# A decoder layer on one core: the place of the cache multiplications, the order and key layout of the prompt scores, and the spacing of x in SBUF

## The chip, the cores and the metric

The kernel runs on one core of a Trainium2 chip. That core has five engines with queues of their own: TensorE (PE, with the weight loads PEld), VectorE (DVE), ScalarE (ACT), GpSimd (POOL) and SyncE (SP, which here only issues DMAs). The metric is the device time of one execution in microseconds (us); lower is better. The kernel before takes 1733.12 us, the median of three runs.

## The reference

One inference step of one decoder layer, for a prompt of 256 tokens and for 8 samples of 4 tokens each, 288 tokens in all, width 2048, all in fp32. The two groups share the weights. Cut to what matters:

```
z = x @ w_in                       # h, gate_b, gate_c, q, k, v, g_a, g_b from one projection
ya = gate_b * conv3(gate_c * h)    # mixer A
for g, (window, dilation) in enumerate(((128, 1), (512, 4), (2048, 16))):
    out[g], lse[g] = banded_attention(q[g], k[g], v[g], slopes[g], dilation)   # mixer B, 4 heads of 128
yb = sum(softmax(lse over g)[g] * out[g] for g in range(3))
x1 = layernorm(ALPHA*x + (sigmoid(g_a) * (ya @ w_branch_a) + sigmoid(g_b) * (yb @ w_branch_b)) @ w_out)
a, b = split(x1 @ w_up)
y = layernorm(ALPHA*x1 + (silu(conv3(a)) * b) @ w_down)
```

In the prompt, a query of dilation group g meets only keys whose distance is a multiple of the dilation. The samples attend to cached keys and values (2048 positions in the widest group, of which a token needs every 16th). Results are y, the new convolution states and the new caches.

## The kernel before, in words

All activations are kept with features on the partitions: x is a tile of 128 partitions by 16 k-tiles by 288 token columns. To keep fp32 precision, each operand is split in a high and a low part (`split`, L228: ACT copies the high part to fp32r, DVE subtracts it). A product of 128 output features (`product`, L204, `mms`, L217) is a sum over the k-tiles of three matmuls: high weights with high x (L223), high weights with low x (L224), low weights with high x (L225). 303 weight blocks pass through in this way, most of them with 16 k-tiles, 48 matmuls.

Weights flow like this: `prepare` (L179) issues the load of a 1 MB block to one of three `wst` buffers on SP's queue and splits it in two halves of 8 k-tiles (`half_block`, L153), each to one of four `whi` and one of four `wlo` buffers. `w_split` holds the two instructions of the last split made, `w_load[0]` the last load.

The order of the products is: queries, keys and values of the heads, the three parts of mixer A, the two gated branches, w_out, and the feed-forward in three thirds. Other work is slipped in between products:

- `sample_events` (L472) is a list of (product number, action). `cache_load` (L446) issues the load of one of 18 cache tiles of 1 MB each for keys (`ck`) and values (`cv`) on SP's queue, behind the last weight load, `LEAD` products ahead of its use, to one of three `cache` buffers. The tiles 2 to 17 of each are due `TILE_K` or `TILE_V` products apart, in two halves; `weighted` (L451) multiplies a half by queries or probabilities (four `activation`s on ACT at L460, one multiplication on DVE at L464) and reduces it (DVE, L466).
- `prompt_attention` (L353) is a generator; its first stage runs right after a head's last value product. POOL first sorts the values of the groups 1 and 2 by class, that is by position modulo 4 (`v_cls`, L359). PE then computes, for each of two query blocks, the scores of group 0 (L367: 128 or 256 columns) and those of groups 1 and 2 by class (L373: 32-column stationary parts, keys read from the key tile with a step of four elements, that is 16 bytes). Two products later the values and probabilities are transposed, and one product later multiplied.

A scheduler places the instructions on their engines: it sorts them by a simulated timeline, keeping dependences. `behind` (L141) adds an order between two instructions that carries no semaphore. So where the program names an action, and where it stands in an engine's queue, can differ. Every engine works its queue off in order: an instruction that waits holds all behind it.

x is held in `xh` and `xl` (L244): each k-tile has two halves of the columns, `HX` = 145 elements each, 144 of which are tokens, and matmuls take an element from each half in turn. The 145th column of the first third of the feed-forward carries the norm's gain and bias (`x_gb`, matmuls of 290 columns); there are 32 such products, and 169 products with 288 columns of x. `yah` and `yal`, the operands of most other products, hold 288 columns in one piece per k-tile.

The functions that the change touches, and what calls them:

Of the kernel before, what the change touches and what calls it, by code (L numbers as in the profile page):

```python
# [12 lines left out]
F32R = mybir.dt.float32r  # L13
AF = mybir.ActivationFunctionType
ALU = mybir.AluOpType
# [3 lines left out]
P = 128  # L19
D = 2048  # L20
KD = D // P
SEQ = 256
NB, NT = 8, 4
# [5 lines left out]
H = T // 2  # L29
HG = H + 1  # L30
HX = 145
FF = 5632
KF = FF // P
HK = KD // 2
THIRDS = (16, 16, 12)
NG, NH = 3, 4
# [10 lines left out]
NM = NG * P  # L47
NC = 4
# [29 lines left out]
SQ = 32  # L78
# [1 line left out]
TILE_K = 2.75  # L80
VALUES_AT = 64
TILE_V = 2.5
LEAD = 7

# [9 lines left out]
def layer_kernel(ctx: ExitStack, tc: tile.TileContext, ins, outs):  # L96
    nc = tc.nc
    pe, dve, act, pool, sp = nc.tensor, nc.vector, nc.scalar, nc.gpsimd, nc.sync

    big = ctx.enter_context(tc.tile_pool(name="big", bufs=1))  # L100
# [6 lines left out]
    def nm(s):  # L107
        uid[0] += 1
        return f"{s}_{uid[0]}"

    def sb(pl, shape, tag, dt=F32, bufs=None):
        return pl.tile(shape, dt, tag=tag, name=nm(tag), bufs=bufs)
# [4 lines left out]
    def h2(ap):  # L117
        return ap.rearrange("p (h a) -> p h a", h=2)

    def h3(ap):  # L120
        return ap.rearrange("p k (h a) -> p k h a", h=2)
# [5 lines left out]
    def att(cols=512):  # L127
        return sb(ps, [P, cols], "att", bufs=2)
# [12 lines left out]
    def behind(i, after):  # L141

        tc.add_manual_dep(i.ins, after.ins.name, no_sync, reason="pace")
# [7 lines left out]
    w_split = []  # L151
# [89 lines left out]
        pe.matmul(o, zero[:, :P], zero, start=True, stop=True)  # L241


    xh = sb(big, [P, KD, 2, HX], "xh", F32R)  # L244
    xl = sb(big, [P, KD, 2, HX], "xl", F32R)
    x_in = ins["x"].rearrange("p (k t) -> p k t", t=T)
    xs = sb(big, [P, KD, T], "yah")

# [8 lines left out]
    for k0, n, queue in FIRST:  # L257
        k = slice(k0, k0 + n)
# [4 lines left out]
    for k0, n, _ in FIRST:  # L263
        k = slice(k0, k0 + n)
        splits.append(split(xh[:, k, :, :H], xl[:, k, :, :H], xs[:, k].rearrange("p k (a h) -> p k h a", h=2)))
        h = slice(k0 % HK, k0 % HK + n)
# [34 lines left out]
    pa = sb(big, [P, KD * T], "yal")  # L301

    m_dist = [pa[:, :NM], pa[:, NM : 3 * NM]]
    v_cls = pa[:, 3 * NM : 3 * NM + 2 * 2 * P].rearrange("p (c k) -> p c k", c=NC)
    q_0 = pa[:, 3 * NM + 4 * P : 3 * NM + 6 * P].rearrange("p (b k) -> p b k", b=2)
    pa_at = [3 * NM + 6 * P]

    def pa_take(n):
        pa_at[0] += n
        return pa[:, pa_at[0] - n : pa_at[0]]  # L310

    v_two = [pa_take(2 * NG * P).rearrange("p (b d) -> p b d", d=P) for _ in range(2)]
    s_two = [pa_take((b + 2) * P) for b in range(2)]
    xs_flat = xs.rearrange("p k t -> p (k t)")
    q_all = xs_flat[:, : NH * NG * T].rearrange("p (j g t) -> p j g t", j=NH, g=NG)
# [32 lines left out]
    def in_a_row(row):  # L348

        for before, i in zip(row, row[1:]):  # L350
            behind(i, before)

    def prompt_attention(j, qT, kT, vT):  # L353


        q5 = h3(qT)[:, :, :, :P].rearrange("p g r (b u c) -> p g b r c u", b=2, c=2)
        k5 = kT[:, 1:, :SEQ].rearrange("p g (b u c r) -> p r c b g u", b=2, c=2, r=2)
        for g in range(1, NG):
            pool.tensor_copy(  # L359
                v_cls.rearrange("p c (b g u) -> p g c b u", b=2, g=2)[:, g - 1],  # L360
                vT[:, g, :SEQ].rearrange("p (b u c) -> p c b u", b=2, c=NC),
            )
        s3 = [att((b + 1) * P + (b + 1) * 2 * SQ) for b in range(2)]
        row = [last_mm[0]]
        for b in range(2):
            n = (b + 1) * P
            row.append(pe.matmul(s3[b][:, :n], q_0[:, b], kT[:, 0, :n], start=True, stop=True))  # L367
            by_class = s3[b][:, n:].rearrange("p (b g u) -> p g b u", g=2, u=SQ)
            for g in range(1, NG):
                for r in range(2):  # L370
                    for c in range(2):
                        at = slice(SQ * (2 * r + c), SQ * (2 * r + c + 1))
                        row.append(pe.matmul(  # L373
                            by_class[at, g - 1], q5[:, g, b, r, c], k5[:, r, c, : b + 1, g - 1], start=True, stop=True
                        ))
        in_a_row(row)
        s = [s_two[b][:, : (b + 1) * (P + 2 * SQ)] for b in range(2)]
        for b in range(2):
            n = (b + 1) * P
            dve.scalar_tensor_tensor(  # L380
                s[b][:, :n], m_dist[b][:, :n], -SLOPE[0][j] / SCALE, s3[b][:, :n], ALU.mult, ALU.add
            )
            dst, src = (t[:, n:].rearrange("p (b g u) -> p g b u", g=2, u=SQ) for t in (s[b], s3[b]))
            for g in range(1, NG):
                m = m_dist[b][:, g * n : (g + 1) * n].rearrange("p (b u c) -> p b u c", u=SQ, c=NC)[:, :, :, 0]
                dve.scalar_tensor_tensor(dst[:, g - 1], m, -SLOPE[g][j] / SCALE, src[:, g - 1], ALU.mult, ALU.add)
        for b in range(2):
            st = sb(wk, [P, 4], "st", bufs=4)
            dve.reduce_max(st[:, 0:1], s[b], AX.X)
            dve.tensor_scalar_mul(st[:, 1:2], st[:, 0:1], -SCALE)  # L390
            act.activation(s[b], s[b], AF.Exp, bias=st[:, 1:2], scale=SCALE, accum_out=st[:, 2:3])
            dve.reciprocal(st[:, 3:4], st[:, 2:3])
            dve.tensor_scalar_mul(s[b], s[b], st[:, 3:4])
        yield 2
        v = v_two[j % 2]
        pv = [att(NG * P) for _ in range(2)]
        row = [last_mm[0]]
        for n in range(2 * NG):
            out = pv[n // NG][:, n % NG * P : (n % NG + 1) * P]
            src = vT[:, 0, n * P : (n + 1) * P] if n < 2 else v_cls[:, n - 2]  # L400
            row.append(pe.transpose(out, src, ident))
        for n in range(2):
            act.copy(v[:, n * NG : (n + 1) * NG], pv[n].rearrange("p (b d) -> p b d", d=P))
        pt = [sb(ps, [P, (b + 2) * P], "acc") for b in range(2)]
        in_a_row(row + [
            pe.transpose(pt[b][:, c * P : (c + 1) * P], s_two[b][:, c * P : (c + 1) * P], ident)
            for b in range(2) for c in range(b + 2)
        ])
        for sT, t in zip(sT_two, pt):
            act.copy(sT, t)  # L410
        yield 1
        po = att(2 * P)
        row = [last_mm[0]]
        row.append(pe.matmul(h2(po), v[:, 0], sT_old, start=True, stop=False))
        row.append(pe.matmul(po[:, P:], v[:, 1], sT_two[1][:, P : 2 * P], start=False, stop=False))
        for c in range(NC):
            at = slice(c * SQ, (c + 1) * SQ)
            row.append(pe.matmul(
                h2(po)[:, :, at], v[:, 2 + 2 * (c % 2) + c // 2], sT_cls[:, :, at], start=False, stop=c == NC - 1
            ))  # L420
        in_a_row(row)
        o_b = oT.rearrange("p (r b u c) -> p b r c u", r=2, b=2, c=2)
        for b in range(2):
            act.copy(o_b[:, b], po[:, b * P : (b + 1) * P].rearrange("p (r c u) -> p r c u", r=2, c=2))
        split(h2(ybh[:, j])[:, :, :P], h2(ybl[:, j])[:, :, :P], oT.rearrange("p (h a) -> p h a", h=2))
# [25 lines left out]
    def weighted(which, n, half, w):  # L451

        c, (g, b) = cache_tiles[which, n], divmod(n - 2, NB)
        cols = NT * P
        for j in (2 * half, 2 * half + 1):
            e = c[:, j * cols : (j + 1) * cols]
            if j % 2 == 0:
                for t in range(NT):
                    e_t = e[:, t * P : (t + 1) * P]
                    act.activation(e_t, e_t, AF.Copy, scale=w[:, g + 1, j, b * NT + t : b * NT + t + 1])  # L460
            else:
                e3 = e.rearrange("p (t k) -> p t k", t=NT)
                w3 = w[:, g + 1, j, b * NT : (b + 1) * NT].unsqueeze(2).broadcast_to([P, NT, P])
                dve.tensor_tensor(e3, e3, w3, ALU.mult)  # L464
        j = slice(2 * half, 2 * half + 2)
        dve.tensor_reduce(  # L466
            parts[:, g, :, j, b * NT : (b + 1) * NT].rearrange("p k j t -> p j t k"),
            c[:, 2 * half * cols : (2 * half + 2) * cols].rearrange("p (j t k c) -> p j t k c", j=2, t=NT, c=SQ),
            AX.X, ALU.add, apply_transpose=True,
        )  # L470

    def sample_events():  # L472
# [98 lines left out]
        for which, w, first, apart in (("ck", q_s, SCORES_AT, TILE_K), ("cv", sT_w, VALUES_AT, TILE_V)):  # L571
            for n in range(N_CT):
                at = first + n if n < 2 else first + 2 + (n - 2) * apart
                yield at - LEAD, partial(cache_load, which, n)
                if n < 2:
# [32 lines left out]
    for j in range(NH):  # L608
        kT, vT = (kv[:, j % 2, c] for c in range(2))
# [58 lines left out]
    for i in range(KD):  # L668
        ph = product(x)
        h = sb(wk, [P, T], "h", bufs=2)  # L670
        act.copy(h2(h), ph)
        pc = product(x)
        u = sb(wk, [P, UW + 2], "u", bufs=2)
# [176 lines left out]
    for part, nf in enumerate(THIRDS):  # L850
        gh = sb(big, [P, KD, T], "yah", F32R)
        gl = sb(big, [P, KD, T], "yal", F32R)
        for k in range(nf):
            pa = product(x_gb if part == 0 else x)
            u = sb(wk, [P, UW + 2], "u", bufs=2)
            up, us = conv_in(u[:, :UW], R_SF + f * 2 * NB)
            if part == 0:
                pa, b1 = normed(pa)
# [227 lines left out]
```

## Time and profile before

| what | us |
|---|---|
| median of three runs (lowest, highest) | 1733.12 (1732.72, 1734.83) |
| the profiled execution | 1734.33 |
| its span, first to last instruction | 1732.5 |
| first matmul of the first three products after the span's start | 9.4 |
| first scores of the four heads, after the span's start | 116.0, 156.1, 196.1, 236.2 |

The profile is that of one execution. Its rows are read like this: a group row gives line, engine, operation, destination and sources by the program's names, shape, count, then busy us and mean ns of one, then idle time of the engine before them and what ended it. In the instructions in order of time the first two columns are start and duration, and brackets hold idle time before the row and its releaser; neighbours of one kind are merged (x8). A list of waits has who waited for what, the total us, how often, and the longest. A row of a stretch has its bounds and length and, for each engine, busy time and instruction count, then the granted clock, the share of the DMA engines and GB/s. A matmul's record covers its way through the array, so records overlap: the pace is read from start to next start, and the end is modelled. A matmul with both operands in plain fp32 has two records.

### The profile page before, as it was taken

How to read it: one execution, taken by the hardware profiler on the slowest of the kernel's cores; microseconds unless marked ns; L12 is line 12 of the kernel's file. 1: busy time of each engine (PE TensorE's matmuls, PEld its weight loads, DVE VectorE, ACT ScalarE, POOL GpSimd, SP SyncE). 2: the span in 40 equal slices, each digit the busy share in tenths (PEclk: the TensorE clock that was granted, in tenths of full speed). 3: DMA queues.
4: the chain of work that ended last, by engine and by line, in shares of the span. 5: the costliest groups of instructions: out<-in, count | busy, mean ns of one | idle time of the engine just before them, and what ended most of it. 6: DMA issues, size and time to landing. Idle time of an engine off the chain costs nothing.

```text
span 1732.5 us, 33671 instructions
## 1 busy us (share of the span) xinstructions
PE 1712.0 (99%) x14102; PEld 1703.6 (98%) x14102; DVE 1100.5 (64%) x1406; ACT 866.8 (50%) x1402; POOL 259.3 (15%) x420
## 2 busy tenths in 40 slices
PE   9999999999999999999999999999999999999996
PEld 9999999999999999999999999999999999999996
DVE  5485667658766654455688888765555554555554
ACT  5455555446555543344445655544454443344444
POOL 0001010000010000011364333300111100011165
PEclk9999999999999999999999999999999999999998
DMA  9676665565666766688766676666676666766652
GB/s 348 231 264 262 240 240 219 209 240 213 263 243 246 294 267 245 247 312 295 306 249 246 259 273 243 257 254 246 259 273 247 261 246 249 273 256 255 241 202 96
DMA packets 57656, 436.16 MB, mean 252 GB/s; under 512 B 7648, under 2 KB 9696, under 8 KB 17632
## 3 DMA queue, kind: packets, MB, share of 16 engines
q1 hardware_dynamic: 55776, 429.29, 65.2%
q10 hardware_dynamic: 1728, 4.72, 0.7%
q8 instruction: 110, 1.80, 0.4%
q14 instruction: 42, 0.34, 0.1%
HBM read 427.53 MB, written 94.53 MB: 301 GB/s over the span
## 4 chain that ended last, share of the span: by engine, by line
PE 90%; DMA 5%; DVE 3%; issue 1%; ACT 1%; SPq 0%; ACTq 0%; DVEq 0%
PE acc L223 29%; PE acc L225 29%; PE acc L224 29%; DMA cache<-in_cv 4%; DVE wlo L229 1%; PE acc L291 1%; DVE sw L466 1%; DMA dd<-in_w_in 0%; DVE cache L464 0%; ACT yah L812 0%; PE att L495 0%; DVE dd L788 0%; ACT cache L460 0%; PE att L373 0%; PE att L367 0%
## 5 line engine op out<-in xcount | busy, mean ns | idle before, releaser
L229 DVE TENSOR_TENSOR wlo<-wst,whi 128x1024 fp32r<-128x1024 f32 (+2 forms) x584 | 703.9, 1209 | 447.0 <-ACT whi L229 445.6
L229 ACT CAST whi<-wst 128x1024 fp32r<-128x1024 f32 (+2 forms) x584 | 591.0, 1016 | 696.8 <-PE acc L224 632.5
L223 PE MATMUL acc<-xh,whi 128*128 128x288 f32 (+1 forms) x3216 | 921.8, 287 | 0.2 <-ACT whi L229 0.2
L224 PE MATMUL acc<-xl,whi 128*128 128x288 f32 (+1 forms) x3216 | 919.2, 286 | 0.0
L225 PE MATMUL acc<-xh,wlo 128*128 128x288 f32 (+1 forms) x3216 | 916.7, 285 | 1.9 <-DVE wlo L229 1.9
L223 PEld LDWEIGHTS acc<-xh,whi 128*128 128x128 f32 x3216 | 605.2, 188 | 2.3 <-issue 1.8
L225 PEld LDWEIGHTS acc<-xh,wlo 128*128 128x128 f32 x3216 | 605.0, 188 | 2.3 <-DVE wlo L229 2.3
L224 PEld LDWEIGHTS acc<-xl,whi 128*128 128x128 f32 x3216 | 606.4, 189 | 0.0
L225 PE MATMUL acc<-yah,wlo 128*128 128x288 f32 x1216 | 348.2, 286 | 1.6 <-DVE wlo L229 1.6
L224 PE MATMUL acc<-yal,whi 128*128 128x288 f32 x1216 | 347.7, 286 | 0.0
L223 PE MATMUL acc<-yah,whi 128*128 128x288 f32 x1216 | 347.6, 286 | 0.0
L225 PEld LDWEIGHTS acc<-yah,wlo 128*128 128x128 f32 x1216 | 229.8, 189 | 2.5 <-DVE wlo L229 2.5
L224 PEld LDWEIGHTS acc<-yal,whi 128*128 128x128 f32 x1216 | 229.8, 189 | 0.0
L223 PEld LDWEIGHTS acc<-yah,whi 128*128 128x128 f32 x1216 | 229.7, 189 | 0.0
L649 POOL COPY qk_s<-u 128x2 f32<-128x2 f32 x44 | 38.1, 866 | 571.7 <-ACT u L863 448.8
L637 DVE SCALAR_TENSOR_TENSOR cy<-u,prm,cy 128x304 f32<-128x304 f32 x120 | 74.8, 624 | 4.0 <-ACT cy L635 1.0
L466 DVE TRANSPOSE_TENSOR_REDUCE sw<-cache 128x32 f32<-128x1024 f32 x64 | 77.1, 1230 | 0.2
L460 ACT ACTIVATE cache<-cache,dd 128x128 f32<-128x128 f32 x128 | 39.4, 389 | 60.1 <-DMA cache<-in_cv 60.1
L708 POOL TENSOR_TENSOR ya<-ya,dd 128x288 f32<-128x288 f32 x16 | 13.6, 851 | 292.0 <-DVE ya L707 292.0
L464 DVE TENSOR_TENSOR cache<-cache,dd 128x512 f32<-128x512 f32 x32 | 20.7, 686 | 48.5 <-DMA cache<-in_cv 48.5
L460 ACT ACTIVATE cache<-cache,qk_s 128x128 f32<-128x128 f32 x128 | 39.5, 389 | 21.8 <-DMA cache<-in_ck 20.6
L229 ACT CAST yah<-ya 128x288 fp32r<-128x288 f32 x76 | 32.7, 430 | 21.7 <-DVE ya L665 8.3
(190 smaller groups left out, 905.3 us busy)
## 6 DMA issues: line engine op xcount, KB each, us to landing
wst<-in_w_in SPq DMA_DIRECT2D x113, 1024.0 KB, 4.9
wst<-in_w_up SPq DMA_DIRECT2D x88, 1024.0 KB, 4.9
wst<-in_w_down SPq DMA_DIRECT2D x32, 1024.0 KB, 4.9
cache<-in_ck SPq DMA_DIRECT2D x18, 1024.0 KB, 7.4
cache<-in_cv SPq DMA_DIRECT2D x18, 1024.0 KB, 7.8
wst<-in_w_a SPq DMA_DIRECT2D x16, 1024.0 KB, 5.2
wst<-in_w_out SPq DMA_DIRECT2D x16, 1024.0 KB, 4.9
wst<-in_w_down SPq DMA_DIRECT2D x16, 768.0 KB, 4.3
```

What stands on the lines that cost most here:

```text
L223: pe.matmul(out, hi[:, c, :], xh_k, start=k == 0, stop=False)
L224: pe.matmul(out, hi[:, c, :], xl_k, start=False, stop=False)
L225: last_mm[0] = pe.matmul(out, lo[:, c, :], xh_k, start=False, stop=k == nk - 1)
L229: return act.copy(hi, src), dve.tensor_tensor(lo, src, f32(hi), ALU.subtract)
L291: i = pe.matmul(o[b], first_w(term == 2, b, k), xk, start=k == 0 and term == 0, stop=k == KD - 1 and term == 2)
L460: act.activation(e_t, e_t, AF.Copy, scale=w[:, g + 1, j, b * NT + t : b * NT + t + 1])
L464: dve.tensor_tensor(e3, e3, w3, ALU.mult)
L466: dve.tensor_reduce(parts[:, g, :, j, b * NT : (b + 1) * NT].rearrange("p k j t -> p j t k"), c[:, 2 * half * cols : (2 * half + 2) * cols ...
L637: dve.scalar_tensor_tensor(y, u[:, i : i + YW], prm[:, w0 + i : w0 + i + 1], y, ALU.mult, ALU.add)
L649: pool.tensor_copy(dst[:, 0:2], u[:, SEQ : SEQ + 2])
L708: pool.tensor_tensor(m, m, ma[:, i], ALU.add)
```

## The change

Three edits, made together.

Cache halves: `weighted` puts each `activation` behind the last weight split's ACT instruction and each multiplication behind its DVE instruction, and `LEAD` goes from 7 to 4.

Prompt scores: POOL also sorts the keys of groups 1 and 2 by class (`k_cls`), the narrow matmuls read them there without a step, and both wide matmuls come ahead of all narrow ones. The space is taken from the second of two buffers `v_two`; there is one `v` for all heads now.

x: a k-tile takes `XK` = 292 elements (1168 bytes) instead of 290 (1160), and the first starts 2 elements (8 bytes) into the tile. Each of the two tiles grows by 136 bytes a partition.

```
@@ -29,6 +29,7 @@
 HX = 145
+XK = 292
...
-LEAD = 7
+LEAD = 4
...
-    xh = sb(big, [P, KD, 2, HX], "xh", F32R)
-    xl = sb(big, [P, KD, 2, HX], "xl", F32R)
+    def x_tile(name):
+        t = sb(big, [P, 2 + KD * XK], name, F32R)[:, 2:].rearrange("p (k c) -> p k c", k=KD)
+        return t[:, :, : 2 * HX].rearrange("p k (h a) -> p k h a", h=2)
+
+    xh, xl = x_tile("xh"), x_tile("xl")
...
+    k_cls = pa[:, 3 * NM + 6 * P : 3 * NM + 10 * P].rearrange("p (c k) -> p c k", c=NC)
+    pa_at = [3 * NM + 10 * P]
...
-    v_two = [pa_take(2 * NG * P).rearrange("p (b d) -> p b d", d=P) for _ in range(2)]
+    v = pa_take(2 * NG * P).rearrange("p (b d) -> p b d", d=P)
...
-        k5 = kT[:, 1:, :SEQ].rearrange("p g (b u c r) -> p r c b g u", b=2, c=2, r=2)
-        for g in range(1, NG):
-            pool.tensor_copy(
-                v_cls.rearrange("p c (b g u) -> p g c b u", b=2, g=2)[:, g - 1],
-                vT[:, g, :SEQ].rearrange("p (b u c) -> p c b u", b=2, c=NC),
-            )
+        k_b, v_b = (t.rearrange("p c (b g u) -> p g c b u", b=2, g=2) for t in (k_cls, v_cls))
+        for dst, src in ((k_b, kT), (v_b, vT)):
+            for g in range(1, NG):
+                pool.tensor_copy(dst[:, g - 1], src[:, g, :SEQ].rearrange("p (b u c) -> p c b u", b=2, c=NC))
...
             row.append(pe.matmul(s3[b][:, :n], q_0[:, b], kT[:, 0, :n], start=True, stop=True))
-            by_class = s3[b][:, n:].rearrange("p (b g u) -> p g b u", g=2, u=SQ)
+        for b in range(2):
+            by_class = s3[b][:, (b + 1) * P :].rearrange("p (b g u) -> p g b u", g=2, u=SQ)
...
-                            by_class[at, g - 1], q5[:, g, b, r, c], k5[:, r, c, : b + 1, g - 1], start=True, stop=True
+                            by_class[at, g - 1], q5[:, g, b, r, c], k_b[:, g - 1, 2 * c + r, : b + 1], start=True, stop=True
...
+        last = list(w_split)
...
-                    act.activation(e_t, e_t, AF.Copy, scale=w[:, g + 1, j, b * NT + t : b * NT + t + 1])
+                    i = act.activation(e_t, e_t, AF.Copy, scale=w[:, g + 1, j, b * NT + t : b * NT + t + 1])
+                    behind(i, last[0])
...
-                dve.tensor_tensor(e3, e3, w3, ALU.mult)
+                behind(dve.tensor_tensor(e3, e3, w3, ALU.mult), last[1])
```

More of the change, by code (lines that the diff above doesn't have):

```diff
@@ L305, in layer_kernel @@
     q_0 = pa[:, 3 * NM + 4 * P : 3 * NM + 6 * P].rearrange("p (b k) -> p b k", b=2)
-    pa_at = [3 * NM + 6 * P]
+    k_cls = pa[:, 3 * NM + 6 * P : 3 * NM + 10 * P].rearrange("p (c k) -> p c k", c=NC)
+    pa_at = [3 * NM + 10 * P]
     def pa_take(n):
@@ L394, in prompt_attention @@
         yield 2
-        v = v_two[j % 2]
         pv = [att(NG * P) for _ in range(2)]
```

## The prediction

> **What bounds the kernel now.** I read the page first, then the waits of TensorE's two halves, the busy time by stretches, and the instructions in order of time where PE was not full.
>
> ```profile
> span 1732.5 us, 33671 instructions
> PE 1712.0 (99%) x14102; PEld 1703.6 (98%) x14102; DVE 1100.5 (64%) x1406; ACT 866.8 (50%) x1402; POOL 259.3 (15%) x420
> PEclk9999999999999999999999999999999999999998
> PE 90%; DMA 5%; DVE 3%; issue 1%; ACT 1%; SPq 0%; ACTq 0%; DVEq 0%
> ```
>
> PE is busy for 99% of the span at a full granted clock, and it holds 90% of the chain that ended last. Only two things can therefore move the time: a stretch in which PE stands still, or the pace at which its matmuls follow each other. The waits of PE and PEld, and the one stretch of the table by stretches where PE is not full (between the start and the tail), show how little stands still:
>
> ```profile
> PE acc L225 <- DVE wlo L229: 3.5, 5, 1.2
> PEld acc L225 <- DVE wlo L229: 4.8, 6, 1.4
> 470.00:620.00 150.00, 146.21 (x1179) 144.74 (x1178) 103.13 (x123) 79.53 (x144) 7.91 (x16) 1.00 0.64 254
> ```
>
> PE lacks 3.8 us between 470 and 620 us, nearly always for a low half of a weight block (`wlo`, DVE, L229). A matmul's record lasts 0.29 us while the next one normally starts 0.12 us after it, and the interval after each stop is 0.10 us longer than usual, so the loss is larger than the idle time. Summed over the starts of the 1179 matmuls of that stretch, intervals beyond the usual one, it is 5.7 us.
>
> Why the low half is late is seen in one of these stops (SP, ACT, DVE and PE in order of time) and in the list of waits:
>
> ```profile
> 522.16 0.42 SPq L448 DMA_DIRECT2D cache<-in_cv  x1
> 530.42 2.44 ACT L460 ACTIVATE cache<-cache,dd 128x128 f32<-128x128 f32 x8 [7.32 <-DMA cache<-in_cv]
> 530.42 1.29 DVE L464 TENSOR_TENSOR cache<-cache,dd 128x512 f32<-128x512 f32 x2 [4.89 <-DMA cache<-in_cv]
> 532.06 2.37 DVE L466 TRANSPOSE_TENSOR_REDUCE sw<-cache 128x32 f32<-128x1024 f32 x2
> 534.35 1.18 DVE L229 TENSOR_TENSOR wlo<-wst,whi 128x1024 fp32r<-128x1024 f32 x1
> 534.08 0.29 PE L224 MATMUL acc<-xl,whi 128*128 128x288 f32 x1
> 535.59 0.39 PE L225 MATMUL acc<-xh,wlo 128*128 128x288 f32 x1 [1.22 <-DVE wlo L229]
> 535.81 0.29 PE L223 MATMUL acc<-xh,whi 128*128 128x288 f32 x1
> ```
>
> ```profile
> ACT cache L460 <- DMA cache<-in_cv: 60.1, 15, 7.3
> DVE cache L464 <- DMA cache<-in_cv: 48.5, 12, 6.1
> DVE cache L464 <- DMA cache<-in_ck: 20.9, 11, 5.3
> ACT cache L460 <- DMA cache<-in_ck: 20.6, 11, 4.8
> ...
> ACT whi L229 <- DMA wst<-in_w_in: 3.4, 4, 1.4
> ```
>
> The scheduler put both halves' multiplications of a cache tile as early as its own timeline allowed. On the chip the load lands 8.3 us after its issue, and ACT and DVE stand in front of it for 7.3 and 4.9 us with the next weight splits queued behind. Then both halves are worked off at once, 3.7 us of DVE, and PE catches up with the splits.
>
> **The change, part 1: cache halves behind a split, LEAD 7 to 4.** It removes and adds no work; it moves 256 `activation`s, 64 multiplications, and with them 64 reductions, and 36 loads on SP's queue. In the built order the multiplications of one half (4 on ACT, 1 and its reduction on DVE) now follow the split of a whole block, and most loads stand three or four weight loads later in SP's queue. To time it, I laid the new order onto the old trace's times: load n's place among the weight loads gives its issue, its half's place among the splits gives its use. The landing, at 8.3 us, comes 24 to 44 us ahead of the use for all 32 tiles. So the 150 us of waiting for `in_ck` and `in_cv` in the rows above go, a burst on DVE shrinks to half (0.65 + 1.19 us), and the stops of PE with them: -5.6 us of the 5.7.
>
> What it adds: three buffers are now held until the product where they are due, and each load reaches SP's head when the previous user still has its last half to do, 4 x 0.3 on ACT and 0.65 + 1.19 on DVE, some 2 to 3 us. SP waits there, with weight loads queued behind:
>
> ```profile
> SPq L184 <- DVE wlo L229: 1315.0, 267, 12.6
> ```
>
> Those wait on SP anyway, 4.9 us each on average, for a block to be split; the next block comes a product (48 matmuls, 5.9 us) later, so 2 to 3 us fit in front of it. If that cover were gone, the splits behind would be late next, and then PE. Bounds: 0 (the stops return elsewhere) to -5.7.
>
> **Part 2: prompt scores.** Four heads, each with one interruption of the products. The first head's, with the end of the product ahead of it:
>
> ```profile
> 115.48 0.29 PE L225 MATMUL acc<-xh,wlo 128*128 128x288 f32 x1
> 115.60 0.29 PE L223 MATMUL acc<-xh,whi 128*128 128x288 f32 x1
> 115.72 0.29 PE L224 MATMUL acc<-xl,whi 128*128 128x288 f32 x1
> 115.85 0.28 PE L225 MATMUL acc<-xh,wlo 128*128 128x288 f32 x1
> 115.97 0.38 PE L367 MATMUL att<-dd,yal 128*128 128x128 f32 x2
> 116.28 0.43 PE L373 MATMUL att<-dd,yah 128*32 128x32 f32 x16
> 116.64 0.70 PE L367 MATMUL att<-dd,yal 128*128 128x256 f32 x2
> 117.27 0.66 PE L373 MATMUL att<-dd,yah 128*32 128x64 f32 x16
> 117.86 0.39 PE L223 MATMUL acc<-xh,whi 128*128 128x288 f32 x1
> 118.08 0.29 PE L224 MATMUL acc<-xl,whi 128*128 128x288 f32 x1
> ```
>
> From 115.97 to 118.08, less the usual 0.12, it costs 1.99 us, 8.0 in four heads. Two 256-column passes take 0.63 us here (116.64 to 117.27). In the value product they take 0.43, and a contiguous 128-column pass in four column groups is in the chain too:
>
> ```profile
> 84.27 1.01 PE att L495 x32
> 136.99 0.43 PE att L414 x2
> ```
>
> Wide first removes one change from narrow to wide and one back: 0.22 (128 columns) + 0.43 (256) + 0.09 (change: 116.28 less 115.97 and 0.22) + 0.23 (narrow, 32 columns: the 0.36 up to 116.64 less a change) + 0.59 (narrow, 64) + 0.10 (refill, as after a stop) = 1.66, so -0.33 a head. Contiguous keys: four concurrent narrow passes of 64 columns, keys 16 bytes apart, take (0.59 - 0.10) / 4 = 0.12 us; L495's take 1.01 / 8 = 0.13 for 128 contiguous columns. Half of that for 64 columns would save 0.06 x 4, and half as much for 32 columns: 0 to 0.3 a head; I take 0.2, nearer to L495's row, since both are four column groups. Sum 4 x 0.53 = -2.1 us, bounds 0 and -2.5.
>
> The Trainium skill ("SBUF — State Buffer", Specifications (TRN2)) says that SBUF lines are 16 bytes and that a read needs two hits a line for full pace. One key per line breaks that, and the rows above agree.
>
> The eight new copies on POOL (128x256, as L359's) stand ahead of the narrow matmuls. The third product's keys are evicted 4.5 us ahead of the scores:
>
> ```profile
> 111.11 0.39 ACT L617 COPY dd<-acc 128x288 f32<-128x288 f32 x1
> 111.56 1.03 POOL L618 COPY qk_s<-dd 128x96 f32<-128x96 f32 x1 [4.34 <-ACT dd L617]
> 145.82 1.35 POOL L359 COPY yal<-dd 128x256 f32<-128x256 f32 x1 [23.43 <-ACT dd L617]
> ```
>
> In the built order POOL does `k_s` (1.03) and then this copy (1.35 at most), to 113.9; the first narrow matmul is due at 116.3. Cost 0, cover 2.4 us; beyond it every us late is a us of PE, four times. The single `v` instead of two: its reads end 1.5 us after 136.99, and the next head's begin six products (35 us) after this one's: 0.
>
> **Part 3: x.** No instruction changes, only where the k-tiles start: 1160 bytes apart from a line's start, so even k at 0 and odd k at 8 bytes into a 16-byte line; afterwards all at 8. All other tiles move by 320 bytes, which keeps their place in a line. The groups concerned:
>
> ```profile
> L224 PE MATMUL acc<-xl,whi 128*128 128x288 f32 x2704 | 772.8, 286 | 0.0
> L224 PE MATMUL acc<-xl,whi 128*128 128x290 f32 x512 | 146.4, 286 | 0.0
> L224 PE MATMUL acc<-yal,whi 128*128 128x288 f32 x1216 | 347.7, 286 | 0.0
> ```
>
> Taking the starts of all rows of L223, L224 and L225 by the parity of k, start to next start: 288 columns, even k 121.7, 122.1, 122.5 ns (366.3), odd k 123.3, 125.0, 121.7 (370.0), mean 368.1; 290 columns, even 123.3 thrice (370.0), odd 125.8, 122.5, 122.5 (370.8), mean 370.4. `yah`, whose tiles all start alike: 122.5 thrice (367.5). So the parity shows, and the trace has no row for a stream of odd starts alone. Ends, per three matmuls: all at 121.7 (288) and 122.5 (290): -3.1 x 2704 - 2.9 x 512 = -9.9 us. All at the worst, 125.0 and 125.8: +18.6 + 3.6 = +22 us. Between them I take the row that is uniform, `yah`, and 290's even pace: -0.6 x 2704 - 0.4 x 512 = -1.9 us. My reason is that at 290 columns an odd start is slow only directly after the change of parity and then runs at 122.5, below the even ones; the slow interval reads as the change, which vanishes.
>
> **Sum.** -5.6 - 2.1 - 1.9 = -9.6 us on the span of 1732.5; the profiled execution took 1734.3, 1.8 more. The runs' median is 1733.1, so 1723.5.
>
> **Rivals.**
> - The odd triple as it stands, 370.0 and 370.8, for every k: +1.9 x 2704 + 0.4 x 512 = +5.3 instead of -1.9, 1730.7. For it: it is the only row with this start. Against it: the order of the intervals at 290 columns. By the Trainium skill ("SBUF — State Buffer", Specifications (TRN2)) each new 16-byte line costs, and an odd start reads 37 + 37 lines at 288 columns against 36 + 37: the rule speaks for this rival and against the change.
> - Slower: reads of x that start at 8 hold 125.0 in a row. It is the second odd interval at 288, sharp to the ns, and in the trace no third one follows that could show more. The gain of parts 1 and 2 is gone from 368.1 + 7.7 / 2.704 = 370.9 a triple; at 375 it is +18.6, 1744. Against it: 290's second odd interval is 122.5.
> - The fast end, 121.7 throughout: 1715.5.
> - Part 1 doesn't do what it says (SP's waits for the held buffers make splits late, or the stops move elsewhere): 1729.1 with the rest. For it: ACT already waits four times for the landing of a weight block, 3.4 us in all.
>
> **Chances.** Forecast 0.36, fast end 0.10, odd triple 0.22, slower 0.20, no gain from part 1 0.12. 0.2% is 3.5 us, about what can be told from no change here. Faster by more: the first two, a fifth of the third, half of the last, 0.56; slower: the slow case and 0.02 of the last, 0.22; within: 0.22. The range, 1713 to 1740, reaches from past the fast end to the lower part of the slow case; the forecast's own is 1720 to 1727.
>
> **What would show it.** Part 1: PE full between 470 and 620 us, no wait for `in_ck` or `in_cv` on ACT and DVE, SP waiting for the reductions instead. Part 2: a score section of 1.5 us, no wait for POOL in it. Part 3: intervals of x without parity, near 122.5; at 123.3 the first rival holds, at 125 the second. A PE wait for `wst` through late splits would make part 1 wrong.

## The result and the profile after

The changed kernel takes 1726.18 us, the median of five runs (1725.15 to 1726.30), beside 1733.12 (1732.56 to 1734.83) for the kernel before: a ratio of 0.9958, 95% interval 0.9943 to 0.9973. In a later series it took 1725.40 (five runs, 1725.14 to 1725.57) beside 1733.61, 0.9953 (0.9941 to 0.9966). The gain is 7 to 8 us, and 1726.18 lies inside the forecast's own range of 1720 to 1727, 2.7 us above its 1723.5.

The profiled execution took 1726.30, with a span of 1724.5. From its page (span, busy time, shares of the chain that ended last):

```profile
span 1724.5 us, 33680 instructions
PE 1707.4 (99%) x14102; PEld 1702.2 (99%) x14102; DVE 1105.9 (64%) x1406; ACT 869.7 (50%) x1402; POOL 272.3 (16%) x428
PE 99%; ACT 0%; DVE 0%; DMA 0%; ACTq 0%; issue 0%; DVEq 0%
```

PE now holds 99% of the chain, where it had 90% with 5% for DMA and 3% for DVE. The span shrank by 8.1 us. The changed kernel's lines are up to five further down: the main matmuls are L224 to L226, the wide scores L370, the narrow ones L377, the split L230, and of the cache halves the load is L451, the multiplications L464 (ACT) and L469 (DVE), the reduction L471.

**Part 1.** The stretch that was not full, from the table by stretches (PE, PEld, DVE, ACT, POOL busy, then clock, DMA share, GB/s):

```profile
470.00:620.00 150.00, 150.00 (x1227) 150.00 (x1226) 109.80 (x126) 85.60 (x155) 4.33 (x14) 1.00 0.76 276
```

PE is full, and 1227 matmuls fit in where 1179 did. The list of waits has no row any more of ACT or DVE for `in_ck` or `in_cv`. These are what is left that could matter, all waits of PE for another engine's data among them:

```profile
SPq L185 <- DVE wlo L230: 1342.8, 283, 7.0
SPq L451 <- DVE sw L471: 42.0, 24, 2.5
ACT whi L230 <- DMA wst<-in_w_in: 9.8, 7, 3.0
PE acc L242 <- DVE cy L239: 1.2, 1, 1.2
PE acc L295 <- ACT yal L230: 0.4, 1, 0.4
```

The wait has moved to SP, as forecast: 24 loads wait for a reduction, at most 2.5 us. ACT's waits for a weight load grew from 3.4 to 9.8 us, but no PE wait follows from them; both PE rows belong to the warm-up and the first three products. DVE's instructions in order of time, in the stage of the stop shown before:

```profile
526.61 1.22 DVE L230 TENSOR_TENSOR wlo<-wst,whi 128x1024 fp32r<-128x1024 f32 x1
527.77 0.53 DVE L665 TENSOR_TENSOR ya<-cy,acc 128x256 f32<-128x256 f32 x2
528.78 1.23 DVE L230 TENSOR_TENSOR wlo<-wst,whi 128x1024 fp32r<-128x1024 f32 x1 [0.48 <-ACT whi L230]
529.93 0.69 DVE L469 TENSOR_TENSOR cache<-cache,dd 128x512 f32<-128x512 f32 x1
530.53 0.45 DVE L230 TENSOR_TENSOR yal<-ya,yah 128x288 fp32r<-128x288 f32 x1
530.90 1.24 DVE L471 TRANSPOSE_TENSOR_REDUCE sw<-cache 128x32 f32<-128x1024 f32 x1
532.06 1.18 DVE L230 TENSOR_TENSOR wlo<-wst,whi 128x1024 fp32r<-128x1024 f32 x1
```

One half at a time, right behind a split, with no bracket for a load: 0.69 and 1.24 us between splits instead of a wait of 4.89 and then 1.29 and 2.37 in one burst.

**Part 2.** The first head's scores, PE in order of time:

```profile
116.92 0.28 PE L226 MATMUL acc<-xh,wlo 128*128 128x288 f32 x1
117.04 0.82 PE L370 MATMUL att<-dd,yal 128*128 128x128 f32 x4
117.79 0.56 PE L377 MATMUL att<-yal,yah 128*32 128x32 f32 x32
118.28 0.39 PE L224 MATMUL acc<-xh,whi 128*128 128x288 f32 x1
118.51 0.29 PE L225 MATMUL acc<-xl,whi 128*128 128x288 f32 x1
```

From the first wide matmul to the product's second one it takes 1.465 us instead of 2.111 (both to the ns, from the starts). In four heads that is 2.6 us less.

**Part 3.** A product of 48 matmuls with 288 columns of x takes 5884 ns from start to start, the median of 169, where it took 5891; with 290 columns 5920 instead of 5927; `yah`'s stays at 5880. That makes 169 x 7 + 32 x 7 ns = 1.4 us. The parity of k no longer shows. But the intervals are not uniform at 288 columns: 121, 122 and 125 ns, with the 125 at every third or fourth matmul, whatever k.

The three parts sum to 5.7 + 2.6 + 1.4 = 9.7 us. From the first main matmul (L224) to the last the trace gains 9.5 us (1680.5 after 1690.0), so that the medians of part 3 give about 0.2 too much: 1.3 is left for it there. The span fell by 8.1, and the rest is at the ends: the first main product starts at 26.34 us instead of 25.21, and the time from the last main matmul to the end is 17.63 instead of 17.34. Both are taken up below.

### The profile page after: what moved, and what is told of

It is laid out like the page before. It is cut to its first block, busy times and chain, and to the rows that moved or that the text cites. A ratio compares the mean times of both kernels' runs of the same rounds, so it can differ in the third digit from the quotient of the medians.

```text
span 1724.5 us, 33680 instructions
## 1 busy us (share of the span) xinstructions
PE 1707.4 (99%) x14102; PEld 1702.2 (99%) x14102; DVE 1105.9 (64%) x1406; ACT 869.7 (50%) x1402; POOL 272.3 (16%) x428
## 4 chain that ended last, share of the span: by engine, by line
PE 99%; ACT 0%; DVE 0%; DMA 0%; ACTq 0%; issue 0%; DVEq 0%
PE acc L224 32%; PE acc L225 32%; PE acc L226 32%; PE acc L295 1%; ACT yah L817 0%; DMA yah<-in_x 0%; DVE dd L793 0%; PE att L500 0%; PE att L421 0%; PE att L404 0%; PE att L370 0%; PE acc L409 0%; PE att L377 0%; PE att L530 0%; PE att L417 0%; PE att L757 0%
## 5 line engine op out<-in xcount | busy, mean ns | idle before, releaser
L230 DVE TENSOR_TENSOR wlo<-wst,whi 128x1024 fp32r<-128x1024 f32 (+2 forms) x584 | 707.2, 1211 | 489.0 <-ACT whi L230 485.3
L230 ACT CAST whi<-wst 128x1024 fp32r<-128x1024 f32 (+2 forms) x584 | 593.3, 1016 | 782.8 <-PE acc L225 713.9
L224 PE MATMUL acc<-xh,whi 128*128 128x288 f32 (+1 forms) x3216 | 918.4, 286 | 0.0
L226 PE MATMUL acc<-xh,wlo 128*128 128x288 f32 (+1 forms) x3216 | 916.7, 285 | 0.0
L224 PEld LDWEIGHTS acc<-xh,whi 128*128 128x128 f32 x3216 | 605.1, 188 | 1.4 <-issue 0.8
L226 PEld LDWEIGHTS acc<-xh,wlo 128*128 128x128 f32 x3216 | 605.1, 188 | 0.0
L226 PE MATMUL acc<-yah,wlo 128*128 128x288 f32 x1216 | 347.7, 286 | 0.0
L224 PE MATMUL acc<-yah,whi 128*128 128x288 f32 x1216 | 347.6, 286 | 0.0
L226 PEld LDWEIGHTS acc<-yah,wlo 128*128 128x128 f32 x1216 | 229.8, 189 | 0.0
L224 PEld LDWEIGHTS acc<-yah,whi 128*128 128x128 f32 x1216 | 229.7, 189 | 0.0
L471 DVE TRANSPOSE_TENSOR_REDUCE sw<-cache 128x32 f32<-128x1024 f32 x64 | 79.7, 1245 | 5.2 <-ACT cache L464 1.1
L464 ACT ACTIVATE cache<-cache,qk_s 128x128 f32<-128x128 f32 x128 | 43.2, 392 | 0.0
L464 ACT ACTIVATE cache<-cache,dd 128x128 f32<-128x128 f32 x128 | 42.1, 390 | 0.0
L665 DVE TENSOR_TENSOR ya<-cy,acc 128x256 f32<-128x256 f32 x88 | 23.3, 303 | 28.1 <-PE acc L226 28.1
L230 ACT CAST yah<-ya 128x288 fp32r<-128x288 f32 x76 | 32.5, 427 | 15.8 <-DVE ya L670 8.1
```

What stands on the lines that cost most here:

```text
L224: pe.matmul(out, hi[:, c, :], xh_k, start=k == 0, stop=False)
L226: last_mm[0] = pe.matmul(out, lo[:, c, :], xh_k, start=False, stop=k == nk - 1)
L230: return act.copy(hi, src), dve.tensor_tensor(lo, src, f32(hi), ALU.subtract)
L464: i = act.activation(e_t, e_t, AF.Copy, scale=w[:, g + 1, j, b * NT + t : b * NT + t + 1])
L471: dve.tensor_reduce(parts[:, g, :, j, b * NT : (b + 1) * NT].rearrange("p k j t -> p j t k"), c[:, 2 * half * cols : (2 * half + 2) * cols ...
L665: dve.tensor_tensor(a, b, c, ALU.mult)
```

## The experiments

The times stand against runs of the kernel before on the same chip. Starts are read to the ns from the traces.

### Each part alone, and a second place for x

The first three runs carry one part of the change each, with that part's lines of the diff above. The fourth has the spacing of x alone, but without the 8 bytes, that is with `XO = 0` here:

```
-        t = sb(big, [P, 2 + KD * XK], name, F32R)[:, 2:].rearrange("p (k c) -> p k c", k=KD)
+        t = sb(big, [P, XO + KD * XK], name, F32R)[:, XO:].rearrange("p (k c) -> p k c", k=KD)
```

> Only the cache halves' edit: multiplications behind a split, LEAD 4; the rest as before. Theory (the halves waited for their loads with weight splits behind them): PE busy for the whole of 470 to 620 us, no wait for in_ck or in_cv on ACT and DVE, -5.6 us, about 1727.5. Rival (the stops of PE come back elsewhere as waits for weight splits): PE lacks 3 us or more in other stretches, 0 to -2 us.

> Only the prompt scores' edit: wide matmuls first and class-ordered keys; the rest as before. Theory: the section from the first wide matmul to the next product's second main matmul falls from 2.1 to about 1.5 us in each of four heads, -2.6 us in all, about 1730.5; the stops of PE between 470 and 620 us stay (146.2 of 150). Rival (the sections shrink, but GpSimd's copies delay the values' or a later stage): less than -1 us, with a wait for POOL on PE.

> Only the spacing of x: k-tiles 1168 bytes apart, the first 8 bytes into a line; the rest as before. Theory: 48 matmuls of a product of x take 5884 ns instead of 5891, -1.4 us in all, too little for the times to tell, about 1731.7; first main product again within 0.3 us of 25.2 us if the 1.1 us that it came later in the changed kernel was that execution's own. Rival (the later start belongs to the spacing of x): first main product near 26.3 us, no gain.

> Only the spacing of x, but with the first k-tile at the start of a line: k-tiles 1168 bytes apart, all at 0 of a 16-byte line. Theory A (the change of parity was the cost, any uniform start does): a product as with the 8-byte start, 5884 ns, -1.4 us. Theory B (the even starts are the fast ones, as the intervals of before had it: 366.3 ns a triple, 370.0 at 290 columns): a product of 16 x 366.3 = 5861 ns, 30 less than before, -5.1 us, and intervals of 121.7, 122.1, 122.5 without a 125.0. Theory C (starts at 8 bytes are the better ones): a product above 5891 ns.

| kernel | median us | before | ratio (95%) | seen in the trace |
|---|---|---|---|---|
| cache halves alone | 1728.78 | 1733.21 | 0.9975 (0.9964 to 0.9985) | no stop of PE, 470 to 620 us full |
| scores alone | 1731.05 | 1733.21 | 0.9988 (0.9979 to 0.9997) | section 1.46 us in each head |
| x at 8 bytes alone | 1731.66 | 1733.21 | 0.9993 (0.9985 to 1.0002) | product 5885 and 5920 ns |
| x at 0 alone | 1732.12 | 1733.21 | 0.9992 (0.9983 to 1.0000) | product 5880 and 5920 ns |

The first two do alone what they do in the changed kernel. The medians' differences, 4.4, 2.2 and 1.6 us, sum to 8.1. For x alone the intervals reach 1, so the times don't show its gain; the products in the traces do.

Part 1 brings 5.7 us in the profiled executions (span 1726.9 after 1732.5) but 4.4 between medians. That fits the stops that it removes, which differ from one execution to the next; the profiled one of before, 1734.33, lies 1.1 above the median. Summed over the intervals of PE between 470 and 640 us beyond the usual one, in every profiled execution whose cache halves are as before: 5.7 (before), 7.1 (scores alone), 4.2 (x at 8), 7.1 (x at 0), 6.6, 4.2 and 4.1 us (three of the next section). The one of 7.1 with the scores alone was the slowest of that kernel's 11 runs, 1733.65 beside a median of 1731.05. The rows of that stretch show how far it goes, first of x at 8, then of x at 0, where the code of the cache work is the same:

```profile
470.00:620.00 150.00, 147.44 (x1192) 146.16 (x1191) 103.69 (x124) 80.64 (x145) 7.91 (x16) 1.00 0.65 260
```

```profile
470.00:620.00 150.00, 146.47 (x1169) 144.96 (x1168) 103.61 (x124) 80.14 (x145) 6.55 (x16) 0.99 0.65 254
```

With x at 0 theory B fell: the even starts do not keep their 121.7. A product takes 5880 ns, as with `yah`, nearly all of it in intervals of 122 and 123, without any 125. So the fast intervals of even k were not to be had without the slow ones of odd k. The turns themselves do cost: 5891 ns with both starts by turns is more than either start takes alone, 5880 and 5885. That much of theory A holds, but its size does not, 11 ns a product at 0 and not 7, and the last section of runs shows that not any uniform start does. The spacing of 1168 bytes came with every one of these starts and was not varied by itself.

In both runs with x alone the first main product starts at 25.18 and 25.11 us: its late start in the changed kernel does not come from the spacing of x.

### Halves of part 1 and of part 2

Two runs split part 1: `behind` with `LEAD = 7`, and `LEAD = 4` without `behind`. Two split part 2: the wide matmuls ahead of the narrow ones with the old keys, and the class-ordered keys (with the single `v`) in the old order of matmuls. The edits are those lines of the diff.

> The cache multiplications behind a split, but LEAD stays 7. In the built order the buffers hold most loads back anyway: 27 of 36 stand at the same weight load as with LEAD 4, 9 stand one to three weight loads earlier. Theory (the order behind a split alone removes the stops): PE 150.00 of 150.00 us between 470 and 620, no wait for in_ck or in_cv on ACT and DVE, about 1728.8 as with both. Rival (LEAD 4 is needed, since loads that stand ahead of their buffer's release hold the weight loads): PE waits for weight splits, 2 us or more over the run with both.

> LEAD 4 alone, multiplications where the scheduler puts them. In the built order a half still stands 4.5 to 5 weight loads ahead of its load's place, as before. Theory: the waits of ACT and DVE for in_cv stay (about 60 and 48 us in all), PE lacks 2.5 to 5 us between 470 and 620 as before, within 1.5 us of 1733.2. Rival (the later loads alone cure it): waits for in_cv below 10 us, PE full, near 1729.

> Wide matmuls first, keys still read with a step of 16 bytes. Theory (one change from narrow to wide and one back fewer): the section of a head falls from 2.11 to 1.78 us, -0.33 each, -1.3 us in all. Rival (it is the keys): 2.0 to 2.1 us.

> Class-ordered keys, order of the matmuls as before. Theory: four concurrent narrow passes take 33 ns instead of 55 at 32 columns and 57 instead of 115 at 64, so the section falls from 2.11 to 1.79 us, -0.32 each, -1.3 us in all. Rival (the gain of the changed kernel came from the order): above 2.0 us.

`behind` with LEAD 7 takes 1729.09 us beside 1733.46, 0.9970 (0.9959 to 0.9982), as with both. `LEAD` 4 alone takes 1734.08, 1.0000 (0.9990 to 1.0009). The stretch of the first of them:

```profile
470.00:620.00 150.00, 150.00 (x1226) 150.00 (x1225) 108.82 (x127) 84.88 (x153) 4.67 (x16) 1.00 0.76 280
```

And of LEAD 4 alone, the stretch and the waits of the cache multiplications:

```profile
470.00:620.00 150.00, 145.55 (x1172) 143.83 (x1171) 103.65 (x125) 79.91 (x148) 7.90 (x16) 1.00 0.64 251
```

```profile
ACT cache L460 <- DMA cache<-in_cv: 63.9, 15, 8.1
DVE cache L464 <- DMA cache<-in_cv: 53.6, 14, 7.0
DVE cache L464 <- DMA cache<-in_ck: 32.2, 14, 6.0
ACT cache L460 <- DMA cache<-in_ck: 21.9, 14, 5.6
```

So the order behind a split is the whole of part 1. Later loads alone cure nothing: in the built order a half still stood 4.5 to 5 weight loads ahead of its load's place, and the waits stay. The order behind a split does two things at once, it ends the waits and it works off one half at a time; no run separates the two.

The scores, with the wide matmuls first and the old keys, PE in order of time:

```profile
115.84 0.82 PE L367 MATMUL att<-dd,yal 128*128 128x128 f32 x4
116.59 0.91 PE L374 MATMUL att<-dd,yah 128*32 128x32 f32 x32
117.43 0.39 PE L223 MATMUL acc<-xh,whi 128*128 128x288 f32 x1
117.66 0.29 PE L224 MATMUL acc<-xl,whi 128*128 128x288 f32 x1
```

And with the class-ordered keys in the old order:

```profile
115.68 0.38 PE L366 MATMUL att<-dd,yal 128*128 128x128 f32 x2
116.00 0.33 PE L372 MATMUL att<-yal,yah 128*32 128x32 f32 x16
116.26 0.70 PE L366 MATMUL att<-dd,yal 128*128 128x256 f32 x2
116.89 0.43 PE L372 MATMUL att<-yal,yah 128*32 128x64 f32 x16
117.25 0.39 PE L223 MATMUL acc<-xh,whi 128*128 128x288 f32 x1
```

By the starts the sections take 1.82 and 1.79 us instead of 2.11: 0.29 for the order, 0.32 for the keys, 0.61 of the 0.65 of both. Each of the two kernels ran once, 1731.54 and 1731.57 us beside 1733.46, too few for the times to say more. The keys' gain is read row against row: the first 16 narrow matmuls take 0.26 us (116.00 to 116.26) instead of 0.36, the second 16 take 0.36 (116.89 to 117.25) instead of 0.59.

### Where in a line x starts, and the changed kernel again

The last four runs are the changed kernel itself, and the changed kernel with the first k-tile 0, 1 or 3 elements into the tile instead of 2, that is at 0, 4 and 12 bytes of a line, with every k-tile at the same place.

> The changed kernel once more. Theory (the first main product's start at 26.3 us and the tail of 17.6 us in its first profile were that execution's own): first main product near 25.2 us, tail near 17.35, span near 1723, and runs between 1724 and 1727 in two clusters about 1.1 us apart. Rival (the three edits together move the start-up or the tail): 26.3 and 17.6 us again, every run above 1725.

> The changed kernel with the k-tiles of x at 0 of a 16-byte line instead of 8. Theory: no interval of 125, every product of 48 matmuls of 288 columns at 5880 ns as that start gave alone, 169 x 4 ns = 0.7 us less than the changed kernel's 5884, 290 columns unchanged at 5920, in all 0.7 us under the changed kernel's next run; too little for the times to tell. Rival (the slips of 125 come from the rest of the changed kernel): 5884 again.

> The changed kernel with the k-tiles of x 4 bytes into a line. Each matmul reads two halves of 144 elements (36 lines' worth), the second 4 bytes further into a line than the first. Theory L (the number of lines read decides: 36 + 37 at a start of 0, 37 + 37 at 8): 37 + 37 here, slips of 125 about every third or fourth matmul, 5884 to 5886 ns a product. Rival S (only a start at 8, the middle of a line, slips): 5880. At 290 columns every start reads 37 + 37 and both expect 5920.

> The changed kernel with the k-tiles of x 12 bytes into a line, so that the second half starts at 0. Theory L (lines): 37 + 36, as many as with a start at 0, no slips, 5880 ns a product. Rival S' (the first half's start must be at 0): slips of 125, 5884 ns or more. Theory on the times: within 1 us of the other three.

| start in the line | median us | ratio (95%) | product, 288 columns | intervals, ns | product, 290 |
|---|---|---|---|---|---|
| 8 (the changed kernel) | 1725.40 | 0.9953 (0.9941 to 0.9966) | 5886 | 121, 122, 125 | 5920 |
| 0 | 1724.62 | 0.9950 (0.9937 to 0.9962) | 5880 | 122, 123 | 5920 |
| 4 | 1724.66 | 0.9949 (0.9935 to 0.9962) | 5880 | 124 or 125, then 121 or 122 twice | 5920 |
| 12 | 1727.00 | 0.9963 (0.9950 to 0.9975) | 5894 | 121, 122, 125 or 126 | 5920 |

The stretch from 620 to 1300 us, mostly products of x, gives the same order in matmuls done. First the changed kernel (its first profile), then 0, then 12 bytes:

```profile
620.00:1300.00 680.00, 680.00 (x5552) 679.68 (x5551) 457.35 (x575) 340.24 (x522) 142.56 (x187) 1.00 0.72 263
```

```profile
620.00:1300.00 680.00, 680.00 (x5553) 679.68 (x5552) 456.35 (x573) 341.06 (x523) 143.03 (x187) 1.00 0.71 264
```

```profile
620.00:1300.00 680.00, 680.00 (x5548) 679.68 (x5547) 457.49 (x575) 340.42 (x523) 143.06 (x187) 1.00 0.70 263
```

12 bytes loses 169 x 14 ns = 2.4 us against 0, and the medians differ by 2.4, where it was expected within 1 us of the other three. It is also slower than the turns of 0 and 8 before, 5894 ns to 5891: one start for every k is not enough. Theory L, by the number of lines read, is refuted on both counts: 4 bytes, which reads 37 + 37 lines, is as fast as 0 (its intervals do slip, at every third matmul, but the two behind give the time back), and 12 bytes, with 37 + 36, is the slowest. Rival S falls too, as 12 bytes slips more than 8, and rival S', as 4 bytes costs no more than 0. What the four runs show is an order, 0 and 4, then 8, then 12; why is open.

The starts at 0 and 4 bytes are the best versions found. They stand 0.7 us below the changed kernel, near the 169 x (5886 - 5880) ns = 1.0 us of the starts, and less than the times alone can tell.

The late first product was that execution's own in the main: the repeat starts it at 25.52 us, the other three at 25.00, 25.35 and 25.68, and the nine kernels with one part or none at 24.92 to 25.69. What happened in the first execution shows in PE's rows in order of time, from the warm-up matmuls (L242) on:

```profile
1.22 4.69 PE L242 MATMUL acc<-cy 128*128 128x288 f32 x18 [1.22 <-DVE cy L239]
...
7.94 0.45 PE L295 MATMUL acc<-xh,whi 128*128 128x288 f32 x1
8.18 0.69 PE L295 MATMUL acc<-xl,yal 128*128 128x288 f32 x2
8.66 0.45 PE L295 MATMUL acc<-xl,whi 128*128 128x288 f32 x1
...
10.34 0.60 PE L295 MATMUL acc<-xh,cache 128*128 128x288 f32 x2
10.78 0.29 PE L295 MATMUL acc<-xh,wlo 128*128 128x288 f32 x1
10.90 0.41 PE L295 MATMUL acc<-xh,yal 128*128 128x288 f32 x2
```

and in the repeat:

```profile
1.22 4.26 PE L242 MATMUL acc<-cy 128*128 128x288 f32 x18 [1.22 <-DVE cy L239]
...
7.05 0.41 PE L295 MATMUL acc<-xh,yal 128*128 128x288 f32 x2
7.30 0.28 PE L295 MATMUL acc<-xh,whi 128*128 128x288 f32 x1
7.42 0.41 PE L295 MATMUL acc<-xl,yal 128*128 128x288 f32 x2
```

Two matmuls come every 0.48 us (8.66 less 8.18) until 10.6 us in the first execution. In the repeat the pace doubles within the warm-up, at 4.9 us by the starts, and these 18 matmuls end 0.43 us sooner; from 7.05 on two come every 0.25 us. In the other twelve profiles the pace doubles somewhere between 4.3 and 7.4 us. Between these two executions the first main product differs by 0.8 us. The Trainium skill ("TensorE: Matmul & The Clock Gate", Part 1: The HAM clock gate) says that TensorE starts at half clock and is released after a busy window of about 3.4 us that runs freely, so that the moment of release varies from run to run. The spread of 4.3 to 7.4 us over 13 profiles agrees with that; that the first execution needed one window more is likely, not shown. The granted clock of the stretch from 7 to 10 us reads 1.00 in both traces, so that only the pace shows the release. In the first series four of the five runs have spans of 1724.3 to 1724.5 and one 1723.3; only one of them was profiled, so that the other three had the same late release is likely, not shown.

The longer tail is not scatter: 17.62 to 17.64 us in all five profiles with the whole change. Of the parts, only the kernel with the class-ordered keys in the old order has the 0.29 us too; all others have 17.33 to 17.35. The last work of ACT ends 4.53 us before the end instead of 4.24, and in between GpSimd's last two semaphore instructions start 0.37 to 0.38 us apart instead of 0.08. The scores alone, with the same keys and the new order, do not have it, so neither edit by itself decides; why this changes at the other end of the program is open.

## Why the prediction was right, and where its terms were off

**Part 1, -5.6 us.** The mechanism held in every step: no waits for the loads, SP waiting for the reductions (at most 2.5 us, where 2 to 3 were allowed), PE full, and no new wait of PE. In the profiled pair it is 5.7. Off was the step from one execution to the median: the stops come from landings, which vary, and the medians give 4.4 (interval of the ratio: 2.6 to 6.2). The working also treated `LEAD` and `behind` as one; `behind` alone does it.

**Part 2, -2.1 us; measured -2.6.** Of the two terms a head, the order was given 0.33 and measured 0.29; its working takes a change of shape as 0.09 us in one term and 0.13 in the next (0.36 less 0.23), and with 0.09 in both it comes to 0.29. The keys were given 0.2, from the row of another matmul, and measured 0.32. The eight new copies of GpSimd cost nothing: in the first head the last copy of keys ends at 114.7 us, 3 us ahead of the narrow matmuls, and the one wait for POOL in the scores is 0.3 us of a weight load (L377), for a copy of queries (L616), once in four heads. The bound of -2.5 was just passed.

**Part 3, -1.9 us; measured -1.4 and -1.1 by the medians in two profiles of the changed kernel, and -1.3 and -1.2 by what is left of the gain between the first and the last main matmul.** The step that failed is the reason, "the slow interval reads as the change, which vanishes". The parity vanished and 290 columns run at their even pace, 5920. But at 288 columns a start at 8 bytes keeps a slow interval of 125 of its own, at every third or fourth matmul. At a start of 0, where no interval of 125 is left, the gain is 169 x 11 + 32 x 7 ns = 2.1 us, close to the forecast's -1.9; at 12 bytes, just as uniform, it would be none. So a uniform start did not by itself bring `yah`'s pace, and there is luck in it that 8 still gained. What spoke for 8, the 122.5 at 290 columns behind the change, did not hold either: there every start takes 5920. The rivals for this part fell: the odd triple as it stood would have meant 16 x 370.0 = 5920 ns a product at 288 columns, 125 in a row 6000, the fast end 5842; it is 5884.

The prediction set a page's rule on lines ("SBUF — State Buffer", Specifications (TRN2), in the Trainium skill) against this part: the start at 8 reads 37 + 37 lines, the start at 0 fewer. The two starts came out in that order, but the runs at 4 and 12 bytes do not follow the count, so no run here bears out the rule as it was applied.

**The sum.** The parts were forecast at -9.6 and came to -9.5 to -9.7 in the profiled pair; that is partly luck, as part 2 gave more and part 3 less. The medians moved by 6.9, and 8.2 in the later series. What the sum lacked is the step to the median in part 1, 0.3 us of tail that the program itself changed, and 1.1 us of start-up in the first execution. In the repeat the same account is 5.7 + 2.6 + 1.1 - 0.3 (tail) - 0.3 (start-up, 25.52 against 25.21) = 8.8, and its span is 1723.7, 8.8 below 1732.5.

## What to carry to other kernels

A scheduler that sorts by a simulated timeline can put an in-order engine in front of a load that has not landed; a plain order behind work that is known to come later cured it here, and moving the load without moving the work did not. Size such a gain from several executions, since stops that hang on landings cost anywhere between 4.1 and 7.1 us an execution here. Where TensorE is the bound at its usual interval, try every start of its moving operand within a line: 14 ns a product of 48 matmuls are 2.4 us in 169 products here, and neither one start for all nor a count of lines foretold which is best.

## What the runs showed that was not expected

- The start of x within a line changes the mean interval at 288 columns from 122.5 ns (0 and 4 bytes) to 122.6 (8) and 122.8 (12), and at 290 columns not at all (5920 ns a product for all four).
- Slow intervals do not add up as they look: with starts by turns the even k began at 121.7 ns while the odd k had a 125, and with one start at 0 the mean is 122.5 throughout. A triple of fast intervals in a mixed stream was no evidence of a fast start.
- Narrow matmuls in four column groups with keys 16 bytes apart cost 0.23 us more per 16 passes of 64 columns than with keys side by side (0.59 against 0.36).
